# Sums of weight blocks made by adding transfers in DRAM, and the down product of an MLP taken form by form

## The chip, the cores and the metric

The program runs on one core of one Trainium2 chip. The metric is the device time in microseconds (us) of one execution. TensorE (PE) multiplies, VectorE (DVE), ScalarE (ACT) and GpSimd (POOL) do elementwise work, and SyncE (SP) issues nearly all transfers (DMAs). Every engine takes its instructions in the order of its own queue. Inputs, weights and intermediates that do not fit on the chip lie in DRAM.

## The reference

A trunk of two layers on 1024 tokens of width 1024. Cut to what matters:

```python
for i in range(2):
    mix = hgrn2_mixer(x, ...) if i == 0 else conformer_conv_mixer(x, ...)
    x = layer_norm(ALPHA * x + mix, ...)
    ff = square(relu(x @ ffn_w1[i])) @ ffn_w2[i]     # 1024 -> 4096 -> 1024
    x = layer_norm(ALPHA * x + ff, ...)
```

The first mixer is a gated linear recurrence over 8 heads (a projection, a recurrence in chunks, a norm with an output gate, an output projection). The second is a pointwise product, a causal convolution of 31 taps per channel, a norm and a second product. All numbers are float32, and the result must be that of float32.

## The kernel before, in words

**Products.** Each float32 operand is split into a high part (rounded to float32r) and a low part (the rest): ACT casts, DVE subtracts (`Slots.split`, line 67). `product` (line 298) then issues three matmuls of 128x128 by 512 columns: high by high, high by low, low by high.

**The down product by forms.** The second MLP product (hidden by `ffn_w2`) is done with seven block products in place of eight. The hidden layer is cut into 8 units of 512 (`NFC`), and each unit's 2 by 2 blocks of hidden activations and of weights are combined into seven forms, taken in the order `ORDER = (1, 2, 6, 5, 7, 3, 4)`. The forms of the hidden activations are written to DRAM by the up product (`hf`, by `store`, line 754) and loaded as tile `dh`. The forms of the weights are made on the chip, as tile `dw`: `Forms.unit` (line 122) loads a unit's four blocks, and DVE makes four sums (`Forms.add`, line 117: tiles `ds` and `dr`), before each form is split. `down_all` (line 850) works through four sets of two units each (`sets`). For each set and form it computes, for each of four groups `gi` (a half of the tokens and a row block in it), 12 matmuls into a PSUM bank. Banks `z` hold the running sum over forms 1, 6, 7, 4 and banks `w` that over 2 and then 5, 3. After every form of every set DVE adds the bank into the rows `y` (`into`, line 854). In the last set the forms 7, 3, 4 are taken group by group, so that the rows `after` them (`to_conv` in layer 0, `last_norm` in layer 1) can be normed one after the other. Four row blocks of 128 tokens make a half; forms 1, 2 and 4 end in blocks with n = 0 (t = 0, 1), and 6, 5, 7, 3 in blocks with n = 1 (t = 2, 3).

**Weights prepared ahead.** While the first MLP runs, `spare` (line 909) loads a weight block of the second mixer or of the second layer's first MLP product into `next`, splits it into `spare` and writes both parts to DRAM (`ready`), so that later it is loaded already split, by two transfers. `ahead` (line 673) lists 32 such blocks: 24 of the mixer and 8 of `w1`. `Forms.form` calls `spare` for 2 (up product) or 3 (down product) of every 7 forms. A `w1` block is used twice, once per half of the tokens (steps `UA` and `UB`); the 8 prepared ones serve steps 0 and 1 of both halves. Blocks without a prepared form are loaded into `raw` and split on the way.

**The recurrence** (line 449, per head and half of the tokens) ends with ACT writing an output tile `o`, which SP stores to `od`. During heads 4 to 7, and after the last one, `gates` (line 405) norms and gates the heads' outputs; in it POOL does two small operations per row block (lines 418 and 382), and DVE continues with their result.

**The order of the work.** Each engine's queue is ordered when the program is built, by a timeline simulated there (`schedule_with_timeline_sim=True`, line 1279); within that, `SEQ` (line 38) sets the order of steps in the second layer: `P` pointwise products, `N` and `F` the convolution's norm, `S` second product, `UA` and `UB` the up product of the two halves. The convolution's taps run beside it, 18 on DVE and 12 by way of POOL (`convolve`, `convolve_pool`, lines 1044 to 1094).

Of the kernel before, what the change touches and what calls it, by code (L numbers as in the profile page):

```python
# [15 lines left out]
P = 128  # L16
D = 1024
S = 1024
KB = D // P
# [37 lines left out]
class Slots:  # L57


    def __init__(self, nc, vector, slots, raws=None):  # L60
        self.nc, self.vector, self.slots, self.raws = nc, vector, slots, raws
        self.queue, self.todo, self.behind = [], [], []

# [7 lines left out]
    def load(self, pieces=1):  # L71

        src, slot = self.todo.pop(0), self.slots()
        self.queue.append(slot)
        if isinstance(src, tuple):
            for i in range(2):
                self.nc.sync.dma_start(out=slot[:, i].bitcast(F32), in_=src[i])
            yield
            return
        raw = self.raws() if self.raws else slot[:, 1].bitcast(F32)  # L80
        if self.behind:
            self.nc.gpsimd.tensor_copy(out=raw[:, :1], in_=self.behind.pop())
        step = 1024 // pieces
        for i in range(pieces):
            c = slice(i * step, (i + 1) * step)
            self.nc.sync.dma_start(out=raw[:, c], in_=src[:, c])
            self.split(slot, raw, c)
            yield

# [11 lines left out]
class Forms(Slots):  # L101


    def __init__(self, nc, vector, slots, raws, sums, spare=None, rate=0, skip=0):
        super().__init__(nc, vector, slots, raws)
        self.sums, self.spare, self.rate, self.skip, self.made = sums, spare, rate, skip, 0

    def form(self, raw):
        slot = self.slots()
        self.split(slot, raw)  # L110
        self.queue.append(slot)
        self.made += 1
        if self.made > self.skip:
            for _ in range(self.made * self.rate // 7 - (self.made - 1) * self.rate // 7):
                self.spare()
# [116 lines left out]
def body(ctx, tc, d, out):  # L232
# [162 lines left out]


# [52 lines left out]
    def recurrence(h, half, zq, zf, carry):  # L449
# [16 lines left out]
        nc.gpsimd.memset(g_r, 1.0)  # L466
# [88 lines left out]
        nc.sync.dma_start(out=od[h // 4][half][:, :, h % 4 * P : (h % 4 + 1) * P], in_=o)  # L555
        carry[h] = state
# [116 lines left out]
    ahead = [("wpw1", (j, i)) for j in range(KB) for i in (1, 0)] + [("wpw2", (n, k)) for n in range(2) for k in range(4)] + [("w1", (i,)) for i in range(8)]  # L673
# [85 lines left out]
    class Up:  # L759
# [9 lines left out]
        def put(self, hr, m, n, t, src, scale):  # L769
            nc.scalar.activation(t, src, AF.Relu, scale=scale)  # L770
            nc.scalar.activation(hr[:, m, n], t, AF.Square)
            mark[0] = hr[:, m, n, :1]
# [68 lines left out]


    mark = [None]
    sets = [(0, 1), (2, 3), (4, 5), (6, 7)]
# [5 lines left out]
    def down_all(y, fw, fh, copies, after, then=None):  # L850

        zs, xs = bank((0, 1, 2, 3)), bank((4, 5, 6, 7))

        def into(gi, m, n, ps, op=ALU.add):
            half, tb = divmod(gi, 2)
            yv = y[half][:, n * 2 + tb, m * HT : (m + 1) * HT]
            vector.tensor_tensor(out=yv, in0=yv, in1=ps, op=op)
            mark[0] = yv[:, :1]

        def one(gi, f, h, ps, start=True):  # L860
# [5 lines left out]
            product(ps, [(two(hp, tok(q)), two(fp, slice(q * HT, (q + 1) * HT))) for fp, hp in zip(f, h) for q in range(2)], start)  # L866


        place = {1: (0, 0, ALU.add), 2: (0, 0, ALU.add), 6: (0, 1, ALU.add), 5: (1, 1, ALU.subtract), 7: (1, 1, ALU.subtract)}
        place.update({3: (0, 1, ALU.add), 4: (1, 0, ALU.subtract)})  # L870
        def step(gi, i, f, h, z, w, copy=None):
            if i in (2, 5):
                w[gi] = xs()
            ps = w[gi] if i in (2, 5, 3) else z[gi]
            one(gi, f, h, ps, i in (1, 2, 5))
            m, n, op = place[i]
            if copy:
                t = copy()
                nc.scalar.copy(out=t, in_=ps)
                ps = t  # L880
            into(gi, m, n, ps, op)

        for s in sets:
            z, w, last = [zs() for _ in range(4)], [None] * 4, s == sets[-1]
            for i in ORDER[:4] if last else ORDER:
                f, h = fw.take(2), fh.take(2)
                fw.ahead(4)
                fh.ahead(4)
                for gi in range(4):
                    step(gi, i, f, h, z, w)  # L890
        f, h = {}, {}
        for gi in range(4):
            for i in ORDER[4:]:
                if gi == 0:
                    f[i], h[i] = fw.take(2), fh.take(2)
                step(gi, i, f[i], h[i], z, w, copies if i == 7 else None)
# [4 lines left out]
            half, tb = divmod(gi, 2)  # L901
            for end in [after(half, (1 - n) * 2 + tb) for n in range(2)][::-1]:
                if end:
                    end()
# [4 lines left out]
    def spare():  # L909
# [3 lines left out]
        slot, raw = hold  # L913
        if staged:
# [6 lines left out]
        if ahead:  # L921
            name, at = ahead.pop(0)

            nc.gpsimd.tensor_copy(out=raw[:, :1], in_=mark[0])
# [4 lines left out]
    fw = Forms(nc, vector, slots((144, 152, 48, 112, 120), "fw"), raws(run(192, 4, 4)), raws(run(160, 2, 4), "sum"), spare, 2)  # L929
# [36 lines left out]
    for half in range(2):  # L966
        for t in range(NTB):
            nc.sync.dma_start(out=y[half][:, t, :], in_=kept[half][t])
            nc.scalar.activation(y[half][:, t, :], y[half][:, t, :], AF.Copy, scale=ALPHA)
# [18 lines left out]
    dc = ring(run(0, 4, 2), wide_t, "dc")  # L988
# [4 lines left out]
    def plan_conv():  # L993
        for op, i in steps:
# [4 lines left out]
            elif op[0] == "U":  # L999
                wa.plan([ready.get(("w1", (4 * i + j,)), d["w1"][4 * i + j]) for j in range(4)])  # L1000
# [3 lines left out]
    down_all(y, fw, fh, dc, to_conv, plan_conv)  # L1004
# [156 lines left out]
    for op, i in steps:  # L1161
# [19 lines left out]
        else:  # L1181
# [3 lines left out]
            if i == NFC - 1:  # L1185
                fw = Forms(nc, vector, slots([64, 72, 144, 152, 200, 208, 112], "dw"), raws([132, 136, 140, 104, 108, 176, 180, 216], "dr"), raws([192, 196, 184, 188], "ds"))
# [28 lines left out]
    down_all(y, fw, fh, ring(run(0, 4, 2), wide_t, "dc"), last_norm)  # L1215
# [67 lines left out]
```

## Time and profile before

| | |
|---|---|
| median of 3 runs | 2159.1 us (2157.28 to 2162.01) |
| the profiled execution's own time | 2158.64 us |
| its span, first to last instruction | 2156.9 us |
| granted TensorE clock | 0.998 |
| DMA | 396.39 MB, mean 184 GB/s |

The stages, as the trace's PE rows show them: the recurrence and projections up to some 480 us, the output projection and first norm to 570, the first up product to 882, the first down product to 1193, the second layer's mixer and the first half of its up product to some 1570, the second half's to 1840, and the second down product from 1840 to 2144. In rows of instructions the first number is the start, the second the duration, and a bracket gives the engine's idle time before it and what ended it. In rows of groups the count is followed by the busy time in us and the mean duration in ns. In rows of waits stand the total, the number of waits and the longest, in us. In rows of transfers stand the count, the size of one and the median time from issue to landing.

### The profile page before, as it was taken

To read this page: it belongs to the slowest core of one execution; us is meant where nothing else is said; L and a number is where in the kernel's file an instruction comes from. 1 tells how busy PE (TensorE), PEld (TensorE's weight loads), DVE (VectorE), ACT (ScalarE), POOL (GpSimd) and SP (SyncE) were. 2 spreads that over 40 slices of the span, in tenths; PEclk is the share of its full clock that TensorE was granted. 3 is DMA by queue.
4 is the path that set the end of the run, shared out by engine and by line. 5 is a ranking of instruction groups with operands and counts; after the bars stand their busy time and mean duration, and the time that the engine had idled before them with its cause. 6 is when DMAs were issued, how large, how long until landed. Compare 5 with 4: busy or idle time off the path is not lost. (4 is left out here: it accounts for less than half of the span.)

```text
span 2156.9 us, 27191 instructions
## 1 busy us (share of the span) xinstructions
PE 2128.9 (99%) x10256; PEld 1769.4 (82%) x10256; DVE 1610.9 (75%) x2281; ACT 968.6 (45%) x1349; POOL 348.2 (16%) x324
## 2 busy tenths in 40 slices
PE   8999999999999999999999999999999999999997
PEld 7888888888888888888888888778788888888886
DVE  6667898876776666889887899579945344878777
ACT  4222332241256555645443576368653343433333
POOL 0000020021100000000001699089401000000001
PEclk9999999999999999999999999999999999999999
DMA  4101220331347767988873755553465988744422
GB/s 182 64 30 30 86 72 30 114 126 49 108 156 259 248 213 272 345 302 322 307 252 123 263 185 187 205 215 125 149 239 217 345 307 306 274 155 154 143 96 96
DMA packets 134978, 396.39 MB, mean 184 GB/s; under 512 B 12736, under 2 KB 41664, under 8 KB 133312
## 3 DMA queue, kind: packets, MB, share of 16 engines
q1 hardware_dynamic: 134848, 394.67, 51.9%
q8 instruction: 80, 1.31, 0.2%
q14 instruction: 50, 0.41, 0.1%
HBM read 277.18 MB, written 117.44 MB: 183 GB/s over the span
## 5 line engine op out<-in xcount | busy, mean ns | idle before, releaser
L167 PE MATMUL ps<-dw,dh 128*128 128x512 f32 x2688 | 610.6, 389 | 0.0
L167 PEld LDWEIGHTS ps<-dw,dh 128*128 128x128 f32 x2688 | 504.5, 188 | 104.4
L167 PE MATMUL ps<-x1f,fw 128*128 128x512 f32 x1344 | 308.1, 390 | 1.2 <-ACT fw L68 0.8
L167 PEld LDWEIGHTS ps<-x1f,fw 128*128 128x128 f32 x1344 | 251.4, 188 | 53.7 <-ACT fw L68 1.2
L167 PE MATMUL ps<-xa,wa 128*128 128x512 f32 x1152 | 270.5, 393 | 1.6 <-ACT xa L604 1.6
L167 PEld LDWEIGHTS ps<-xa,wa 128*128 128x128 f32 x1152 | 215.0, 189 | 45.7 <-ACT xa L604 2.0
L167 POOL TENSOR_TENSOR cb<-cb,prod 128x512 f32<-128x512 f32 x176 | 240.8, 1377 | 22.2 <-ACT prod L1057 11.5
L167 DVE SCALAR_TENSOR_TENSOR ps<-u,par,ps 128x512 f32<-128x512 f32 x288 | 198.5, 749 | 10.8 <-ACT ps L1067 9.5
L167 PE MATMUL ps<-x0T,wa 128*128 128x512 f32 x768 | 190.3, 398 | 6.3 <-ACT x0T L346 6.3
L167 DVE TENSOR_TENSOR y<-y,ps 128x512 f32<-128x512 f32 x232 | 156.5, 682 | 35.6 <-PE ps L167 35.1
L167 PE MATMUL ps<-xc,wa 128*128 128x512 f32 x768 | 174.2, 389 | 0.0
L382 POOL TENSOR_TENSOR mv<-mv,nhalf 128x1 f32<-128x1 f32 x32 | 44.7, 1399 | 780.5 <-DVE mv L167 780.5
L167 PEld LDWEIGHTS ps<-x0T,wa 128*128 128x128 f32 x768 | 141.9, 189 | 34.7 <-ACT x0T L346 6.3
L167 PEld LDWEIGHTS ps<-xc,wa 128*128 128x128 f32 x768 | 144.2, 188 | 29.9
L68 ACT CAST dh<-dh 128x1024 fp32r<-128x1024 f32 x112 | 117.3, 1052 | 114.5 <-DMA dh<-hf 112.9
L167 DVE TENSOR_TENSOR dh<-dh 128x1024 fp32r<-128x1024 f32 x112 | 136.0, 1222 | 25.3 <-ACT dh L68 24.7
L167 DVE TENSOR_TENSOR wa<-raw,wa 128x1024 fp32r<-128x1024 f32 (+1 forms) x74 | 96.6, 1307 | 75.4 <-ACT wa L68 75.3
L68 ACT CAST wa<-raw 128x1024 fp32r<-128x1024 f32 (+1 forms) x74 | 75.7, 1025 | 161.6 <-PE ps L167 140.1
L1057 ACT ACTIVATE prod<-u,par 128x512 f32<-128x512 f32 x176 | 124.4, 721 | 46.6 <-POOL cb L167 45.9
L167 PE MATMUL ps<-wv,x0T 128*128 128x512 f32 x576 | 142.0, 395 | 0.0
L167 PEld LDWEIGHTS ps<-wv,x0T 128*128 128x128 f32 x576 | 106.0, 188 | 21.3
L68 ACT CAST dw<-dr 128x1024 fp32r<-128x1024 f32 x64 | 67.1, 1052 | 88.3 <-PE ps L167 83.8
(178 smaller groups left out, 2791.7 us busy)
## 6 DMA issues: line engine op xcount, KB each, us to landing
wa<-ready SPq DMA_DIRECT2D x128, 512.0 KB, 4.4
dh<-hf SPq DMA_DIRECT2D x112, 512.0 KB, 4.7
ready<-spare SPq DMA_DIRECT2D x64, 512.0 KB, 3.8
dr<-in_w_dram SPq DMA_DIRECT2D x64, 512.0 KB, 5.3
raw<-in_w_dram SPq DMA_DIRECT2D x48, 512.0 KB, 5.0
raw<-in_w1q_dram SPq DMA_DIRECT2D x36, 512.0 KB, 3.8
hf<-ht SPq DMA_DIRECT2D x64, 256.0 KB, 4.2
hf<-ht SPq DMA_DIRECT2D x32, 512.0 KB, 7.0
```

Source lines behind the costliest of these rows:

```text
L68: self.nc.scalar.copy(out=slot[:, 0, c], in_=raw[:, c])
L167: return op(*args, **kw)
L382: nc.gpsimd.tensor_tensor(out=dst, in0=src, in1=nhalf[:, :n], op=ALU.pow)
L1057: nc.scalar.activation(tp, u[:, k : k + HT], AF.Copy, scale=tap(j, k))
```

## The change

- **Sums in DRAM.** A new helper is called once at the end of each of the 16 recurrence steps, for one of the 16 units (8 per layer). It makes the four sums of the unit's weight blocks in DRAM: two copies on SP's queue, then three transfers on POOL's queue that add into their destination. A transfer of two numbers from `o` goes first, so that the copies start only after that step's output.
- **Down product form by form.** `down_all` runs over forms on the outside and over all 8 units inside; each bank gathers a form over 8 units before DVE adds it into `y`. Each form of the weights is loaded from DRAM, from an input block or a sum, and split (`Slots` in place of `Forms`). Form 4 takes two units for all groups, then the other six group by group. The blocks with n = 1 are normed after form 3, those with n = 0 after each group.
- **Rows loaded later.** `y` (the residual) of layer 0 is loaded and scaled when the third unit of form 1 is taken, not before the down product.
- **Preparing weights.** `ahead` lists 13 `w1` blocks in place of 8, and they are used in `UA` only. `spare` is called for 3 of 8 forms in the up product up to the 43rd, and 5 of 8 in the down product from the 12th to the 55th; its load now follows the split of the form just loaded, by a one-column copy on DVE and one on POOL.
- **Smaller edits.** The memset of `g_r` in the recurrence goes from POOL to ACT. In the last rows, blocks (1,0) and (1,1) in place of (1,1) and (1,3) take the norm by statistics on DVE.

```diff
+    def block_sums(name, layer, c, after):
+        t = sums[name, layer, c] = dram.tile([4, P, 1024], F32, name=f"sum_{name}{layer}{c}")
+        v, w = t.rearrange("a p n -> p a n"), d[name][layer, c].rearrange("a p n -> p a n")
+        nc.sync.dma_start(out=t[0:4:2, 0, 0:1], in_=after)
+        nc.sync.dma_start(out=v[:, 0:2], in_=w[:, 0:4:2])
+        nc.sync.dma_start(out=v[:, 2:4], in_=w[:, 0:2])
+        nc.gpsimd.dma_start(out=v[:, 0:2], in_=w[:, 2:4], accum_op=ALU.add)
+        for i in (2, 3):
+            nc.gpsimd.dma_start(out=v[:, i], in_=v[:, i - 1], accum_op=ALU.add, max_dma_last_dim=4096)
+    def form(name, layer, c, i):
+        w, t = d[name][layer, c], sums[name, layer, c]
+        return {1: w[0], 2: w[1], 6: t[2], 5: t[1], 7: t[0], 3: t[3], 4: w[3]}[i]
...
-        nc.gpsimd.memset(g_r, 1.0)
+        nc.scalar.activation(g_r, f_l, AF.Identity, bias=one, scale=0.0)
...
         nc.sync.dma_start(out=od[h // 4][half][:, :, h % 4 * P : (h % 4 + 1) * P], in_=o)
+        block_sums(*to_sum.pop(0), o[:2, 0, :1])
...
     def plan_down(layer, fw, fh):
-        fw.todo = [[(blocks("w2", layer, c),) for c in s] for s in sets]
-        fh.plan([hf[layer][c][i] for s in sets for i in ORDER for c in s])
+        fw.plan([form("w2", layer, c, i) for i in ORDER for c in range(NFC)])
+        fh.plan([hf[layer][c][i] for i in ORDER for c in range(NFC)])
...
+        for i in ORDER:
+            for c in range(NFC if i != 4 else 2):
+                f, h = fw.take(), fh.take()
+                if c == 2 and i == 1 and first:
+                    first(f[0][:, 1, :1].bitcast(F32))
                 fw.ahead(4)
                 fh.ahead(4)
                 for gi in range(4):
+                    one(gi, i, f, h, c == 0 and i in (1, 2, 5))
+                    if c == NFC - 1:
+                        into(gi, i)
+            if i == 3:
+                rings["aux"] = bank((4, 5))
+                rows = [lambda gi=gi: after(gi // 2, 2 + gi % 2) for gi in range(4)]
+                for _ in range(2 if then else 4):
+                    rows.pop(0)()
+        f, h = fw.take(NFC - 2), fh.take(NFC - 2)
         for gi in range(4):
+            for c in range(0, NFC - 2, 2):
+                one(gi, 4, f[c : c + 2], h[c : c + 2])
+            into(gi, 4)
...
+            end = after(gi // 2, gi % 2)
...
-ahead = [("wpw1", (j, i)) for j in range(KB) for i in (1, 0)] + [("wpw2", (n, k)) for n in range(2) for k in range(4)] + [("w1", (i,)) for i in range(8)]
+ahead = [("wpw1", (j, i)) for j in range(KB) for i in (1, 0)] + [("wpw2", (n, k)) for n in range(2) for k in range(4)] + [("w1", (i,)) for i in range(13)]
...
-    fw = Forms(nc, vector, slots([112, 120, 144, 152, 128, 136, 168], "dw"), raws([192, 196, 200, 204, 160, 164, 64, 68], "dr"), raws([80, 84, 88, 92], "ds"), spare, 3)
+    fw = Slots(nc, vector, slots([112, 120, 144, 152, 128, 136, 168], "dw"), raws([192, 196, 200, 204, 160, 164], "dr"), spare, 5, range(12, 56))
...
-                wa.plan([ready.get(("w1", (4 * i + j,)), d["w1"][4 * i + j]) for j in range(4)])
+                wa.plan([ready.get(("w1", (4 * i + j,)) if op == "UA" else None, d["w1"][4 * i + j]) for j in range(4)])
...
-        if (half, t) not in ((1, 1), (1, 3)):
+        if (half, t) not in ((1, 0), (1, 1)):
```

More of the change, by code (lines that the diff above doesn't have):

```diff
@@ L88, in load, with count @@
             yield
+        self.count(slot)
+    def count(self, slot):
+        if self.spare:
+            self.made += 1
+            if self.made in self.when and self.made * self.rate // 8 > (self.made - 1) * self.rate // 8:
+                self.spare(slot[:, 1, :1].bitcast(F32))
     def ahead(self, n):
@@ L111, in form @@
         self.queue.append(slot)
[L112 to L115, printed above, removed]
+        self.count(slot)
     def add(self, x, y, out=None):
@@ L864, in tok, with into @@
                 return slice(q * HT + half * 256 + tb * P, q * HT + half * 256 + (tb + 1) * P)
[L866 to L875, printed above, removed]
-            m, n, op = place[i]
[L877 to L886, printed above, removed]
+            parts = [(two(hp, tok(q)), two(fp, slice(q * HT, (q + 1) * HT))) for fp, hp in zip(f, h) for q in range(2)]
+            product((w if i in (2, 5, 3) else z)[gi], parts, start)
+        def into(gi, i):
+            half, tb = divmod(gi, 2)
+            m, n, op = place[i]
+            yv = y[half][:, n * 2 + tb, m * HT : (m + 1) * HT]
+            vector.tensor_tensor(out=yv, in0=yv, in1=(w if i in (2, 5, 3) else z)[gi], op=op)
+        for i in ORDER:
[3 more added lines that the diff above has]
+                    first(f[0][:, 1, :1].bitcast(F32))
                 fw.ahead(4)
@@ L900, in down_all, with spare @@
                 then()
[L901 to L904, printed above, removed]
+            end = after(gi // 2, gi % 2)
+            if gi == 1:
+                while rows:
+                    rows.pop(0)()
+            if end:
+                end()
     hold, staged = [], []
-    def spare():
+    def spare(after):
         if not hold:
```

58 lines of the change are left out of this document (26 added, 32 removed).

## The prediction

> **What bounds the kernel now.** I read the page first, then who PE (TensorE) waited for, then stretches of the span (after the stretch: busy us and instruction count of PE, weight loads, DVE, ACT and POOL; granted clock; DMA share; GB/s), then single places.
>
> ```profile
> span 2156.9 us, 27191 instructions
> PE 2128.9 (99%) x10256; PEld 1769.4 (82%) x10256; DVE 1610.9 (75%) x2281; ACT 968.6 (45%) x1349; POOL 348.2 (16%) x324
> ...
> PE ps L167 <- ACT x0T L346: 6.3, 1, 6.3
> PE ps L167 <- DVE cb L167: 3.5, 2, 2.9
> PE ps L167 <- ACT xa L604: 1.8, 3, 1.3
> ...
> 72.00:455.00 383.00, 382.33 (x2333) 323.86 (x2332) 301.74 (x622) 106.77 (x174) 17.63 (x29) 1.00 0.21 67
> ...
> 928.00:1135.00 207.00, 207.00 (x915) 171.47 (x914) 183.75 (x198) 98.06 (x96) 19.43 (x17) 1.00 0.81 287
> ...
> 1839.60:2144.40 304.80, 304.80 (x1345) 252.15 (x1343) 238.86 (x270) 128.66 (x136) 7.24 (x5) 1.00 0.45 153
> ```
>
> PE is the bound nearly everywhere. In the second layer's down product (last row) 1345 matmuls take 304.8 us, 226 ns each, with DVE free for a fifth of the time. The change has the same 1344 matmuls of 512 columns per layer, so neither fewer DVE additions nor fewer DVE sums can shorten that stretch by themselves. What can be won at all is PE's idle time, 2156.9 - 2128.9 = 28 us: the 6.3 at the start, which the change does not touch, about 12.5 at the end, and what is left in the convolution. So I price three places where the end can move: the last rows, the convolution, and the places where new transfers may make PE wait.
>
> **The tail.**
>
> ```profile
> 2139.71 4.70 PE L167 MATMUL ps<-dw,dh 128*128 128x512 f32 x20
> ...
> 2145.64 0.63 DVE L167 TENSOR_TENSOR y<-y,ps 128x512 f32<-128x512 f32 x1
> 2146.19 1.27 DVE L167 SCALAR_TENSOR_TENSOR y<-y,mv,ln_ffn_b 128x1024 f32<-128x1024 f32 x1
> ...
> 2148.77 0.68 DVE L167 BATCH_NORM_STATS2 bs<-y 128x6 f32<-128x512 f32 x1
> 2149.37 1.39 DVE L167 SCALAR_TENSOR_TENSOR y<-y,mv,ln_ffn_b 128x512 f32<-128x512 f32 x2
> 2150.69 0.20 DVE L167 BATCH_NORM_AGGREGATE mv<-bs 128x2 f32<-128x12 f32 x1
> 2150.92 0.15 DVE L167 TENSOR_SCALAR mv<-mv 128x1 f32<-128x1 f32 x1
> 2150.99 1.40 DVE L167 SCALAR_TENSOR_TENSOR y<-y,mv,ln_ffn_g 128x512 f32<-128x512 f32 x2
> 2152.31 1.41 DVE L167 SCALAR_TENSOR_TENSOR y<-y,mv,ln_ffn_b 128x512 f32<-128x512 f32 x2
> ```
>
> Columns: start, duration. PE ends at 2139.71 + 4.70 = 2144.41; DVE ends at 2152.31 + 1.41 = 2153.72, so 9.3 us of DVE follow the last product, because three row blocks are in their norm at once. After the change the four blocks of n = 1 are normed from form 3's end on, beside form 4's 192 matmuls, and block (1,0) runs under the last 36 of them (36 x 0.226 = 8.1 us); behind the last product stands one block: add 0.63, statistics 0.68, 0.20 and 0.15, first pass 1.40, second pass 1.41 (POOL's power lies under the first pass), together 4.5, and some 0.3 for the releases between engines: 4.8. **Gain 4.5.** Bounds: 4.8 without those releases, and 2.0 if two more passes (1.40 + 1.41) still stand ahead of it on DVE. The first of those four groups of 36 also takes six units in 8.1 us, each with two splits of 1.22 on DVE (a row below); the two units ahead of it (48 matmuls, 10.8 us) are the cover, and 6 x 2.44 = 14.6 us fit into 18.9; the norms beside them may push PE back by up to 2, inside the lower bound. The store after it is the same.
>
> **The convolution.** Here w1 blocks 0 to 12 are split in advance instead of 0 to 7, and used in the first half only.
>
> ```profile
> 1540.72 0.39 PE L167 MATMUL ps<-xa,wa 128*128 128x512 f32 x1
> 1544.04 0.66 PE L167 MATMUL ps<-ident,cb 128*128 128x128 f32 x4 [2.93 <-DVE cb L167]
> 1544.45 2.95 PE L167 MATMUL ps<-xa,wa 128*128 128x512 f32 x8
> 1547.20 1.05 PE L167 MATMUL ps<-ident,cb 128*128 128x128 f32 x4
> ...
> 1541.10:1548.00 6.90, 3.97 (x18) 0.81 0.25 77
> ...
> 1432.00:1541.00 109.00, 108.40 (x488) 89.33 (x486) 101.11 (x132) 86.72 (x134) 98.09 (x67) 1.00 0.41 139
> 1545.00:1640.00 95.00, 95.00 (x437) 78.71 (x436) 58.46 (x87) 42.13 (x64) 4.06 (x3) 0.98 0.51 185
> ...
> L167 DVE TENSOR_TENSOR wa<-raw,wa 128x1024 fp32r<-128x1024 f32 x15 | 26.8, 1785 | 3.3 <-ACT wa L68 3.3
> ```
>
> Before 1541 DVE is busy for 101 of 109 us and POOL for 98; PE then stands for the convolution's sums and its clock falls (0.81 in that stretch). From 1541.10 to 1548.00 there are 10 matmuls and 8 transposes: at 226 ns, and 100 ns per transpose (four from 1544.04 to 1544.45), 3.1 us of work in 6.9. So 3.8 are lost, and 3.5 - 2.9 = 0.6 more in an earlier wait for cb. The change takes 13 - 8 = 5 splits out of the first half: 5 x 1.785 = 8.9 us of DVE, more than the wait. **Gain 4.4.** Bounds 0 (POOL's additions end last instead) and 6.2 (the waits for xa, 1.8, too). The second half gains 8 splits, 8 x 1.8 = 14 us at most, in a stretch where DVE is busy for 58 of 95: no cost, and without that cover 14.
>
> **The recurrence.** Each of 16 steps gets on SP's queue one tiny transfer and two copies of 1 MB, and on POOL's one addition of 1 MB and two of 512 KB, each waiting for the one before. POOL stands in its queue at those waits; behind them are the gates' small operations.
>
> ```profile
> 71.82 0.60 ACT L554 ACTIVATE o<-ps 128x512 f32<-128x512 f32 x1 [2.12 <-PE ps L167]
> ...
> 451.98 0.60 ACT L554 ACTIVATE o<-ps 128x512 f32<-128x512 f32 x1
> ...
> 273.63 0.19 POOL L418 TENSOR_SCALAR ss<-ss 128x4 f32<-128x4 f32 x1 [2.23 <-DVE ss L167]
> ...
> 472.00 1.01 POOL L382 TENSOR_TENSOR ss<-ss,nhalf 128x4 f32<-128x4 f32 x1
> ...
> ha<-ha SPq DMA_DIRECT2D x8, 1024.0 KB, 5.3
> ...
> raw<-in_wqf_dram SPq DMA_DIRECT2D x14, 512.0 KB, 3.6
> ...
> od<-o SPq DMA_DIRECT2D x16, 256.0 KB, 2.6
> ...
> y<-in_x_dram SPq DMA_DIRECT2D x2, 2048.0 KB, 8.0
> ...
> 273.28 0.40 ACT L465 COPY G<-F 128x256 f32<-128x256 f32 x1
> ```
>
> First and last of 16 outputs o: a step each (451.98 - 71.82) / 15 = 25.3 us. No row shows an adding transfer. Lower bound, as a plain transfer: tiny 2.6, copies 8.0 at the worst, additions 5.3 and 3.6 until the last is issued: 19.5. Upper, an addition at twice a plain one: 2.6 + 8.0 + 10.6 + 7.2 = 28.4. DMA is busy at 0.21 from 72 to 455, so the room is there, and the sums are first needed after 885. SP's queue stands some 2.6 us per step at the tiny transfer; loads of the next head behind it are a step early. What can cost time is POOL: the gates' operations (16 pairs between 273.63 and 473) sit in POOL's queue between the additions, DVE waits for each of them in its own order, and PE for DVE. The queue's order is fixed at the build by a simulated timeline (line 1279); an addition longer than assumed there holds what follows, by up to 28.4 - 19.5 = 8.9 in each of the four or so steps that share POOL with the gates: 0 to +36. I take **+2**, nearer the lower end, since POOL is busy for 18 of 383 us there. The memset that goes from POOL to ACT lengthens the chain of G by some 0.4, 16 x 0.4 = 6.4 if bare; PE is fed from other products there (382.3 of 383 busy): 0.
>
> The Trainium skill (Collectives: The Full Stack, The bandwidth ceiling) says that an add in the transfer engines reads two sources through one ring and so runs at half a copy's rate; no run here shows it. By that rule the chain would be the upper one, 28.4, longer than a step, and the first rival below decides.
>
> **The first down product.** DVE loses 84 of 112 additions and 32 sums per layer, and gets 7 more splits of weights in advance.
>
> ```profile
> L167 DVE TENSOR_TENSOR y<-y,ps 128x512 f32<-128x512 f32 x232 | 156.5, 682 | 35.6 <-PE ps L167 35.1 <-POOL next L924 0.3
> ...
> L167 DVE TENSOR_TENSOR ds<-ds,dr 128x1024 f32<-128x1024 f32 x32 | 39.0, 1221 | 0.2
> ...
> L167 DVE TENSOR_TENSOR spare<-next,spare 128x1024 fp32r<-128x1024 f32 x32 | 39.1, 1223 | 20.5 <-ACT spare L916 20.4
> ...
> dh<-hf SPq DMA_DIRECT2D x50, 512.0 KB, 6.0
> ...
> SPq L920 <- ACT spare L916: 66.0, 18, 8.6
> SPq L86 <- PE ps L167: 53.1, 24, 9.2
> ```
>
> That is 84 x 0.682 + 32 x 1.22 - 7 x 1.22 = 88 us of DVE per layer here and 96 in the last, all beside a PE that never waits: 0. Accumulation in PSUM across eight units adds no wait, since a bank that DVE reads at the end of a form is written again a form (43 us) later. Transfers grow: a unit and form is 24 x 0.226 = 5.4 us and loads 2 x 512 KB; from the 12th load to the 50th, 207 us, 25 steps of preparing load 512 KB and store 1 MB. 39 x 1.05 + 25 x 1.57 = 80 MB in 207 us is 387 GB/s, where the stretch 928:1135 moved 287 at a share of 0.81, or 354 at a full one. So the queue ends some 9% of 207, 19 us, late. SP now waits for PE to free dh slots (53.1 us), so it runs ahead to the seven slots: six units, 32 us, less 6.0 and 2.3 of split leaves 24 of cover. **0**; without that cover +19.
>
> **Sum.** 2158.64 (this execution's time, 1.7 above its span) - 4.5 - 4.4 + 2 = 2151.7. The median of the runs, 2159.1, is 0.5 higher: **2152**.
>
> **Rivals.**
> *POOL is held in the recurrence* (slower). Place: gates behind an addition; it decides when a chain exceeds what the order allowed by more than about 5 us in four or five steps, 5 x 5 = 25 net of the 2: 2152 + 23 = 2175. For it: PE has no wait to lose there, and every late DVE result becomes a PE wait. Against it: 25.3 us a step against 19.5.
> *Transfers bound the first down product* (slower): the 19 us come without cover, because SP stands at 25 stores instead of 18: 2171. For it: 387 against 354. Against it: the slots.
> *The convolution's wait stays*: POOL's 98 of 109 us are not relieved, so 2152 + 4.4 = 2156.4.
> *The change does not do what it says* at the end: the last block still finds DVE occupied by norms and splits, so its gain is the lower bound or less: 2152 + 4.5 = 2156.5. For it: DVE was busy in the last rows above without a gap. Against it: 84 additions fewer.
>
> **How the numbers follow.** Forecast 0.47 (own range 2146 to 2156), convolution 0.14, tail 0.06, POOL 0.20, transfers 0.13. This measurement tells about 0.2%, 4.3 us, from no change: under 2154.8 is faster, over 2163.4 slower. The forecast gives 0.43 to faster and 0.04 to same; the next two 0.07 and 0.11, with 0.02 slower; the last two 0.33 slower. Together 0.50, 0.15, 0.35. Low end: 2152 with the upper bounds of tail (0.3) and convolution (1.8), nothing lost in the recurrence (2) and 3 won there (POOL's queue without the memset that DVE waits on): 2145. The high end takes in both slower cases at their prices and leaves out the upper part of POOL's bound: 2178.
>
> **What will show it.** Right: PE's last matmul some 8.5 us before the last instruction's end instead of 12.5; no wait for cb over 1 us near the end of the first half's w1; PE busy to 0.5 us in each stretch from 72 to 500; full PE in the first down product at a DMA share above 0.9. Wrong: PE waits for yn or state between 270 and 480, POOL's small operations far behind their DVE releasers, or PE waiting for dw or dh splits between 930 and 1140.

## The result and the profile after

The changed kernel takes 2172.65 us (median of 6, 2170.48 to 2178.47) against 2159.22 us for the kernel before beside it: ratio 1.0065, 95% interval 1.005 to 1.0079. It is slower by 0.65%, and the forecast was 2152, faster. The time lies inside the stated range; the direction is the other one, and the number is 2.4 us from the 2175 of the rival *POOL is held in the recurrence*.

The profiled execution of after took 2172.09 us. Its waits of PE (total, number, longest) and its stretches, columns as in the prediction:

```profile
PE ps L172 <- DVE yn L172: 14.9, 1, 14.9
...
PE ps L172 <- ACT z L1150: 1.8, 2, 1.2
PE ps L172 <- ACT xa L631: 1.4, 1, 1.4
```

```profile
72.00:250.00 178.00, 177.34 (x1059) 150.31 (x1057) 125.93 (x247) 50.98 (x83) 16.57 (x17) 1.00 0.75 189
250.00:400.00 150.00, 149.69 (x928) 126.40 (x927) 135.51 (x294) 46.06 (x82) 28.31 (x33) 1.00 0.85 219
400.00:450.00 50.00, 50.00 (x313) 42.32 (x313) 34.84 (x75) 10.87 (x18) 5.72 (x6) 1.00 1.01 305
450.00:500.00 50.00, 34.38 (x156) 27.92 (x155) 22.58 (x48) 16.95 (x27) 16.87 (x22) 0.83 0.93 259
```

One new wait of 14.9 us, in the only stretch where PE lost its work, and there the clock fell to 0.83. From 72 to 500 us the DMA share is 0.75 and more (0.21 before, up to 455), and from 400 on the engines are full or nearly so (1.01, then 0.93).

Marks set on the first product of each stage show where the time went. In all traces of this study they are read at the same five places; "no sums" and "moved" are the experiments e3 and e12 below.

| us | before | after | no sums | moved |
|---|---|---|---|---|
| start to first x1f,fw (recurrence, output projection, first norm) | 571.87 | 591.57 | 571.95 | 575.65 |
| from there to first xa,wa (first MLP) | 621.53 | 621.05 | 621.00 | 621.03 |
| to the second dw,dh (convolution, second up product) | 646.20 | 645.38 | 645.38 | 645.96 |
| to the last product's end | 304.81 | 304.81 | 304.80 | 304.80 |
| to DVE's last instruction | 9.31 | 4.53 | 4.54 | 4.53 |

So +19.7, -0.5, -0.8, 0, -4.8: together +13.6, and the spans differ by 13.4. All of the loss is in the first row.

What PE waited for is seen on three engines' timelines of after (start, duration, engine, line; the bracket is the idle time before and what ended it). POOL:

```profile
444.84 1.19 POOL L410 DMA_DIRECT2D sum_w<-in_w_dram  x1 [10.90 <-DMA sum_w<-in_w_dram]
457.29 0.86 POOL L412 DMA_DIRECT2D sum_w<-sum_w  x1 [11.26 <-DMA sum_w<-in_w_dram]
466.63 0.81 POOL L412 DMA_DIRECT2D sum_w<-sum_w  x1 [8.48 <-DMA sum_w<-sum_w]
467.25 1.41 POOL L410 DMA_DIRECT2D sum_w<-in_w_dram  x1
483.93 0.86 POOL L412 DMA_DIRECT2D sum_w<-sum_w  x1 [15.26 <-DMA sum_w<-in_w_dram]
484.87 0.19 POOL L444 TENSOR_SCALAR ss<-ss 128x4 f32<-128x4 f32 x1
485.14 1.03 POOL L387 TENSOR_TENSOR ss<-ss,nhalf 128x4 f32<-128x4 f32 x1
```

DVE, then PE:

```profile
465.96 1.28 DVE L172 TENSOR_REDUCE ss<-sq 128x4 f32<-128x512 f32 x2 [8.77 <-ACT sq L441]
...
486.21 1.14 DVE L172 SCALAR_TENSOR_TENSOR yn<-yn,ss,sg 128x128 f32<-128x128 f32 x4 [16.70 <-POOL ss L387]
```

```profile
467.65 4.01 PE L172 MATMUL ps<-wa,x0T 128*128 128x512 f32 x17
486.61 0.74 PE L172 MATMUL ps<-ident,yn 128*128 128x128 f32 x2 [14.95 <-DVE yn L172]
487.00 3.76 PE L172 MATMUL ps<-wa,x0T 128*128 128x512 f32 x8
```

DVE had the sums of squares ready at about 467. POOL's two small operations on them (lines 444 and 387, 1.2 us) stand in its queue behind the second addition of a unit, and that one waits for the first, from 467.25 to 483.9. PE ran out of other products at 471.66. The eight matmuls after the wait take 470 ns each where 226 is usual (granted clock 0.50 from 486.5 to 491). In numbers: the first ident,yn product starts at 439.87 before and 442.70 after (+2.8), the wait is 14.95, and some 2 us more go to the low clock.

The chain of waits of after tells the same from the other end (start, duration, what):

```profile
423.60 12.15 DMA sum_w<-o
435.81 8.64 DMA sum_w<-in_w_dram
...
444.84 11.87 DMA sum_w<-in_w_dram
...
457.29 0.86 POOL sum_w L412
...
467.25 16.28 DMA sum_w<-in_w_dram
...
484.87 0.20 POOL ss L444
...
486.21 0.36 DVE yn L172
486.57 0.04 issue
486.61 121.96 PE ps L172 x587
```

### The profile page after: what moved, and what is told of

Same layout as the page of the kernel before. It is cut to its first block, busy times and chain, and to the rows that moved or that the text cites. A ratio compares the mean times of both kernels' runs of the same rounds, so it can differ in the third digit from the quotient of the medians.

```text
span 2170.3 us, 27318 instructions
## 1 busy us (share of the span) xinstructions
PE 2133.8 (98%) x10256; PEld 1772.7 (82%) x10256; DVE 1452.6 (67%) x2098; ACT 973.4 (45%) x1365; POOL 378.9 (17%) x369
## 2 busy tenths in 40 slices
DMA packets 161349, 494.99 MB, mean 228 GB/s; under 512 B 15040, under 2 KB 43968, under 8 KB 159680
## 3 DMA queue, kind: packets, MB, share of 16 engines
HBM read 370.50 MB, written 189.79 MB: 258 GB/s over the span
## 4 chain that ended last, share of the span: by engine, by line
PE 91%; DMA 4%; DVE 2%; POOL 1%; issue 1%; ACT 1%; SPq 0%; DVEq 0%; POOLq 0%; ACTq 0%
PE ps L172 91%; DMA sum_w<-in_w_dram 2%; POOL cb L172 1%; DMA sum_w<-o 1%; DVE wa L172 0%; DMA raw<-in_w_dram 0%; DVE ps L172 0%; DMA raw<-in_wg_dram 0%; DMA raw<-in_wv_dram 0%; DMA raw<-in_wqf_dram 0%; DVE wv L172 0%; DMA raw<-in_xT_dram 0%; DMA raw<-in_w1q_dram 0%; ACT wv L69 0%; ACT wa L69 0%
## 5 line engine op out<-in xcount | busy, mean ns | idle before, releaser
L172 DVE TENSOR_TENSOR dw<-dr,dw 128x1024 fp32r<-128x1024 f32 x112 | 136.6, 1222 | 110.6 <-ACT dw L69 110.0
L69 ACT CAST dw<-dr 128x1024 fp32r<-128x1024 f32 x112 | 117.4, 1052 | 133.1 <-PE ps L172 124.8
L172 DVE TENSOR_TENSOR wa<-raw,wa 128x1024 fp32r<-128x1024 f32 (+1 forms) x77 | 96.8, 1258 | 88.6 <-ACT wa L69 88.2
```

Of the source, the lines that this page charges most:

```text
L69: self.nc.scalar.copy(out=slot[:, 0, c], in_=raw[:, c])
L172: return op(*args, **kw)
```

## Experiments

Times are medians; each has its interval against the kernel before on the same chip where it matters. "Mark" means the first row of the table, which is 571.9 before and 591.6 after; it and the waits come from the one profiled execution of a run, which can lie some us from the median. "Marker" is the transfer of two numbers that goes ahead of a unit's copies. Two explanations compete in the expectations below. *Hold*: POOL stands at the wait of an addition, with the gates' operations behind it in its queue. *Traffic*: the DMA engines are full, so that o and yn come late whatever POOL does.

### What in the recurrence costs: the sums, their adding, or their bytes

**e3, no sums.** The call is dropped; forms 6, 5, 7 and 3 load plain blocks.

```diff
-        block_sums(*to_sum.pop(0), o[:2, 0, :1])
...
-        return {1: w[0], 2: w[1], 6: t[2], 5: t[1], 7: t[0], 3: t[3], 4: w[3]}[i]
+        return {1: w[0], 2: w[1], 6: w[2], 5: w[1], 7: w[0], 3: w[3], 4: w[3]}[i]
```

> Leaves the sums out: forms 6, 5, 7 and 3 of the second weights take plain input blocks; all else is the changed kernel. If the sums in the recurrence are the whole loss: span before 450 us as in the kernel before, no wait for yn, tail and convolution as in the changed kernel, total 2152 to 2155. If the rest of the change (forms one by one, marks of the spare work, copies) costs as well: 2157 or more.

2152.38 us (2151.6 to 2153.36), ratio 0.9972 (0.9962 to 0.9982), mark 571.95. All of the loss comes from making the sums; the rest of the change is worth 6.7 us.

**e4, plain copies.** POOL's three transfers per unit lose `accum_op=ALU.add`; queue, chain, places and sizes stay, and the adding is left out.

> Leaves the adding out: POOL's three transfers per unit write the same places by plain copies, same queue, same chain, same bytes moved to the destination. If the hold is long because an addition takes about half as long again as a copy (10.4 against 6.8 us for 1 MB): the three transfers of the last units end some 8 to 10 us earlier, PE's wait for yn falls to 3 to 7 us, total 2160 to 2165. If it is long because each waits for the one before on full DMA engines, adding or not: the wait stays at 11 to 15 us, total 2168 to 2173.

2153.55 us, ratio 0.998 (0.9971 to 0.999), mark 574.03: better than either expectation. The queues and issues of after, then of e4 (packets, MB, share of 16 engines; then count, size, median us from issue to landing):

```profile
q0 software_dynamic: 8960, 33.56, 8.7%
...
sum_w<-in_w_dram POOLq DMA_DIRECT2D x16, 1024.0 KB, 10.4
sum_w<-sum_w POOLq DMA_DIRECT2D x32, 512.0 KB, 5.5
```

```profile
q0 software_dynamic: 8960, 33.56, 4.5%
...
sum_w<-in_w_dram POOLq DMA_DIRECT2D x16, 1024.0 KB, 7.0
sum_w<-sum_w POOLq DMA_DIRECT2D x32, 512.0 KB, 3.8
```

The same packets and bytes hold the engines for 8.7% of 2170.3 us instead of 4.5% of 2151.9: 188.8 against 96.8 us of all 16, a factor of 1.95, or 178 against 347 GB/s. That is the price that the prediction left open between 1 and 2. The Trainium skill (Collectives: The Full Stack, The bandwidth ceiling) says that an add runs at half a copy's rate because it reads two sources. The rate is what this pair of runs shows; the reason is not, since the profile's page counts the same reads from memory in both (370.50 MB).

**e2, gates off POOL.** The additions stay; the second gates' two small operations go to DVE and ACT.

```diff
+            if n == 0:
...
+            else:
+                vector.tensor_scalar(out=ss[:, 1], in0=ss[:, 0], scalar1=1.0 / P, scalar2=RMS_EPS, op0=ALU.mult, op1=ALU.add)
+                nc.scalar.activation(ss[:, 1], ss[:, 1], AF.Sqrt)
+                vector.reciprocal(ss[:, 0], ss[:, 1])
```

> All sums stay where the changed kernel makes them; only the second gates' two small operations leave POOL's queue (DVE multiplies and adds, ACT takes the root, DVE the reciprocal). Hold theory: POOL stands as long as in the changed kernel (its additions near 457, 467 and 484 us), but nothing of PE waits for it; PE's wait for yn falls from 14.9 to under 3 us, total 2154 to 2159. Traffic rival (yn's loads from DRAM are late behind full queues, whichever engine does the gates): the wait stays above 8 us, total 2164 to 2171.

2160.09 us, ratio 1.0024 (1.0009 to 1.0038). The executions fall in two groups, four from 2159.3 to 2160.1 and three from 2167.3 to 2168.4; the profiled one is of the upper. In it the wait for yn is gone, and another stands in its place:

```profile
473.09 1.15 ACT L441 ACTIVATE sq<-yn 128x512 f32<-128x512 f32 x2 [14.00 <-DMA yn<-od]
480.62 0.60 ACT L438 ACTIVATE sg<-ps 128x512 f32<-128x512 f32 x1 [6.38 <-issue]
```

```profile
481.99 6.09 PE L172 MATMUL ps<-wa,x0T 128*128 128x512 f32 x14 [11.92 <-DVE sg L172]
```

ACT stands 14 us for yn's load from DRAM, and then 6.38 more before `sg`, for which PE waits; that the profile puts down to nothing ("issue"). In after, the same instruction waited for the store of the last o:

```profile
467.00 0.60 ACT L438 ACTIVATE sg<-ps 128x512 f32<-128x512 f32 x1 [0.55 <-DMA od<-o]
```

In e2 that store is issued at 459.44, and SP issues the load of yn that needs it at 480.56, just before `sg` starts. So it is most likely this store, some 21 us under way, that PE waits for; no run shows it alone. Two things then end close together: POOL's hold, and o's way through DRAM to yn on full engines. Taking the first away wins some 12 us in one group and 5 in the other, of which only the second has a trace. Both theories had a part: the hold is the longer of the two, the traffic the one right behind it.

### Which units

**e6, last three copied; e7, only the last three added.** In e6 units 5 to 7 of layer 1 are copied without adding, in e7 the other thirteen.

```diff
+        op = {"accum_op": ALU.add} if (layer, c) < (1, 5) else {}
-        nc.gpsimd.dma_start(out=v[:, 0:2], in_=w[:, 2:4], accum_op=ALU.add)
+        nc.gpsimd.dma_start(out=v[:, 0:2], in_=w[:, 2:4], **op)
```

> Leaves the adding out for the last three units alone (plain copies at the same places); thirteen units are added as in the changed kernel. Local theory (only the additions beside the loads of yn and y at 400 to 490 us cost): PE's wait for yn falls under 2 us, total 2153 to 2157. Backlog theory (each addition is a little late, and the lateness of thirteen adds up to the hold): the wait stays at 8 us or more, total 2164 to 2172.

> The reverse: thirteen units are plain copies, the last three are added. Local theory: PE's wait for yn stays at 10 to 16 us, total 2166 to 2173. Backlog theory: the wait falls under 3 us, total 2153 to 2158.

e6: 2169.49 us (two executions near 2163, three near 2170; the profiled one waits 7.6 for yn and 2.7 for sg). e7: 2162.43 us (seven from 2159.8 to 2164.4, three from 2169.0 to 2170.4; 7.0 for sg). Neither theory holds alone: the last additions cost some 9 us by themselves (e7 against e4), and earlier ones make even plain copies late (e6). The stores of o in after say why it is the end. SP's queue:

```profile
379.93 0.56 SPq L581 DMA_DIRECT2D od<-o  x1
399.21 0.56 SPq L581 DMA_DIRECT2D od<-o  x1
422.98 0.57 SPq L581 DMA_DIRECT2D od<-o  x1
442.20 0.57 SPq L581 DMA_DIRECT2D od<-o  x1
...
455.03 0.56 SPq L581 DMA_DIRECT2D od<-o  x1
```

The last steps are 19.3, 23.8, 19.2 and 12.8 us long, not the mean of 25.3, and in them the residual's 4 MB are loaded too. A unit whose additions alone take 10.4 and 5.5 us at the median, and up to 16.3 there, is started every 12.8 to 23.8 us: the units pile up just where the second gates need POOL.

### Moving the last three units

**e1, in the first up product.** Called after units 5 to 7 of that product, marked by a weight slot.

```diff
-        block_sums(*to_sum.pop(0), o[:2, 0, :1])
+        if len(to_sum) > 3:
+            block_sums(*to_sum.pop(0), o[:2, 0, :1])
...
+        if c >= NFC - 3:
+            block_sums(*to_sum.pop(0), f[:2, 1, :1].bitcast(F32))
```

> The sums of the last three units (layer 1, c 5 to 7) are made in the first up product, the other thirteen in the recurrence as in the changed kernel. Hold theory (the additions of the last units stand ahead of the second gates' two small operations in POOL's queue, and PE stands 14.9 us for yn behind them): the wait of PE for yn falls under 1.5 us, PE keeps its clock there, first x1f,fw product 16 to 19 us earlier than 591.6, total 2153 to 2157. Traffic rival (the transfers as such keep yn's loads and POOL late): a wait of 8 us or more stays, total 2164 to 2171. Rival that the added bytes cost wherever they are put: the up product takes as much longer as the recurrence saves, total 2168 to 2173.

2170.71 us; no wait for yn, mark 576.82, but the first MLP takes 638.5 instead of 621.0 (the profiled execution took 2174.84 us). The last rival's number came out, yet not because bytes cost everywhere:

```profile
PE ps L172 <- ACT dh L69: 5.0, 1, 5.0
PE ps L172 <- DVE c L172: 3.9, 1, 3.9
PE ps L172 <- ACT c L823: 2.7, 2, 2.0
```

They met the loads of weights prepared ahead and the first loads of dh, for which ACT stands in order (11.0 us for dh at 889.66).

**e5, in the second down product, unmarked; e8, the last three unmarked at their old place.** Both leave the marker out for these units; the edit shown is e8's.

```diff
-        nc.sync.dma_start(out=t[0:4:2, 0, 0:1], in_=after)
+        if (layer, c) < (1, 5):
+            nc.sync.dma_start(out=t[0:4:2, 0, 0:1], in_=after)
```

> The sums of the last three units are made in the second down product during its first form, which needs none of them (the share of the DMA engines there was 0.56 and POOL has next to nothing to do), without a marker transfer. Hold theory with a local cause: no wait of PE for yn, none in the first up product, the recurrence loses 2 to 5 us, the second down product nothing: total 2153 to 2157. Rival that the additions' bytes cost wherever they are put: PE waits for dw or dh in the second down product for 8 us or more, total 2163 to 2172.

> The marker transfer is left out for the last three units, so that SP does not stand some 12 us until it has landed and the copies start at once after the store of o. If the wait for the marker is part of the hold's length: the last additions end 8 to 12 us earlier, PE's wait for yn falls to 3 to 7 us, total 2160 to 2165. If the transfers are bound by the DMA engines, which are full from 400 to 490 us, the order in which they are issued changes little: wait 11 to 16 us, total 2168 to 2174.

2164.43 and 2165.69 us. Neither tested what it was made for: with nothing to wait for, the three units' additions ran at 24 to 75 us in both, whatever their place in the program, since the build's simulated timeline orders the queues. There they delayed a small load, and in e8

```profile
54.52 0.72 DVE L172 COPY_PREDICATED at<-mask,ps 128x512 f32<-128x512 int32 x1 [9.83 <-DMA mask<-in_mask_dram]
```

so that PE stood 7.4 us for qn (6.7 in e5). The wait for yn was gone in both: with the last units away, the hold is too. Without a marker nothing pins a unit to its place.

**e9, in the second down product, marked.** As e5, with `f[0][:2, 1, :1]` as marker.

> As e5, but with a marker transfer from the weight slot in use, so that the three units start in the second down product and not elsewhere. If the hold of POOL in front of the second gates is the loss: wait for yn under 1 us, first x1f,fw product at 573 to 577 us, second down product without waits, total 2153 to 2157. Rival that the second down product has no room for them (three units of about 18 us of all engines in its first 87 us): PE waits for dw or dh 5 us or more, total 2160 to 2170.

2170.38 us. Mark 577.08, first MLP 621.04, but 661.2 in the convolution and second up product: two units were issued at 1685 to 1728 us, ahead of the down product, and PE stood 6.1 and 2.0 us for wa there. (Of the 15.8 us more in that row, 3.8 are products of the down product taken early: its own row is that much shorter.) A place that is free by its own share says nothing of the one where the transfer is issued.

**e12, in the second up product.** After blocks 1, 3 and 5 of its first half; in the recurrence as in e1.

```diff
...
             up_half(1, i, 0, wa, stA, x3T[0])
+            if i in (1, 3, 5):
+                block_sums(*to_sum.pop(0), wa.queue[0][:2, 1, :1].bitcast(F32))
```

> The last three units are made in the first half of the second up product, one after every second block, where POOL has 7 us of work in 300 and the DMA engines' share is 0.72. If the hold in front of the second gates is the loss and traffic costs nothing where there is room: no wait for yn, none in the second up product, total 2153 to 2157. If the share rises to 1 there and weights come late: 2160 to 2170.

2156.87 us, ratio 1.000 (0.999 to 1.0009): 15.8 us less than after, with the same transfers. No wait for yn; last column of the table. This is the clearest proof that the last three units, at their place, were most of the loss. 3.7 us of the first row stay.

### The 4 us that stayed

**e13, layer 0's sums alone,** in the first eight steps (the second layer's are left out). **e15,** e12 with all gates off POOL as in e2.

```diff
+        if to_sum[0][1] == 0:
             block_sums(*to_sum.pop(0), o[:2, 0, :1])
```

> Sums of layer 0 alone, made in the first eight steps of the recurrence, before any gate; the second layer's forms 6, 5, 7 and 3 take plain input blocks (its sums are left out). Hold theory (additions cost only where the gates' operations stand behind them): first x1f,fw product at 572 to 573 us, total 2152 to 2154. Traffic theory (each unit costs some 0.25 us wherever it stands in the recurrence): 574 us and later, total 2154.5 to 2157.

> As e12 (thirteen units in the recurrence, three in the second up product), with the two small operations of all gates off POOL's queue (DVE, ACT root, DVE reciprocal). Hold theory: first x1f,fw product at 572 to 573.5 us instead of 575.7, total 2153 to 2155. Traffic theory: it stays at 575 to 577, total 2156 to 2158.

2156.61 and 2158.8 us (e15: ratio 1.000), marks 577.69 and 576.51: the hold theory misses both. e15 weighs less, since its square root makes ACT load function tables 20 times in place of twice, 1.28 us each. e13 shows that this loss arises before any gate. ACT in e13, what it stood for:

```profile
87.33 1.05 ACT L69 CAST wv<-raw 128x1024 fp32r<-128x1024 f32 x1 [4.98 <-DMA raw<-in_wv_dram]
...
242.18 1.05 ACT L69 CAST wv<-raw 128x1024 fp32r<-128x1024 f32 x1 [11.15 <-DMA raw<-in_wg_dram]
```

In e3 the same two places show 1.2 and 4.0. The units started after steps 0 and 5 (stores of o at 72.6 and 223.6) run just ahead of two bursts of weight loads; ACT's casts come late, then DVE's splits, and PE stands 2.7 us for qn at 242.9.

**e16, none after steps 0 and 5.** Eleven units in the recurrence; five in the last pointwise block and after blocks 1, 3, 5 and 7.

```diff
+        if 2 * h + half not in (0, 5, 13, 14, 15):
             block_sums(*to_sum.pop(0), o[:2, 0, :1])
```

> Eleven units in the recurrence (none after steps 0 and 5, which stand ahead of the two bursts of weight loads, none after the last three), five in the last pointwise block and the second up product. If weights that come late behind these two units are what is left of the loss: no wait of PE for qn over 0.3 us, first x1f,fw product at 572 to 573.5 us, total 2152.5 to 2155, faster than the kernel before. If every unit costs a little wherever it stands: 574.5 us and more, total 2155.5 to 2159. If five units are too many for the end of the convolution: waits for cb, z or xa there, total above 2158.

2161.71 us, ratio 1.0018 (1.0009 to 1.0027). Mark 573.16 and no wait of PE between 72 and 400 us: that was most of the recurrence's remaining loss (e3: 571.95). But the convolution takes 653.6 us instead of 645.4:

```profile
PE ps L172 <- DVE cb L172: 7.9, 2, 6.2
```

POOL makes cb there, and additions between its taps are the same hold in another place: POOL stood 5.4 and 3.0 us before the issues at 1494 and 1514.

**e17, two of those later:** after blocks 1, 3, 5, 6 and 7.

> Eleven units in the recurrence as in e16, five in the second up product after blocks 1, 3, 5, 6 and 7. If e16's loss in the convolution was the unit in the last pointwise block: no wait for cb over 1.5 us, total 2152.5 to 2155.5, faster than the kernel before by 0.1 to 0.25%. Rival that units closer together than some 30 us hold each other and the weights up there: waits in the second up product or for cb, total 2156 to 2162.

2161.18 us (2157.91 to 2165.0), ratio 1.0015. Mark 573.56 again, 653.0 after it: 2.9 us for cb and 3.2 for a wa loaded already split. Its rival held.

**e14, layer 1's units in the convolution:** five among the pointwise blocks, three as in e12, layer 0's in the first eight steps.

> All sixteen sums: layer 0 in the first eight steps of the recurrence, layer 1 in the convolution (after every second pointwise block, five units) and in the second up product (three units, as in e12). If only the hold in front of the gates costs: total 2152 to 2155, faster than both kernels. Rival: the convolution's own work on POOL (46 of 50 us busy there) stands behind the additions, PE waits for cb or xa: 3 us or more in the convolution, total 2157 to 2166.

2167.83 us, ratio 1.0046. The convolution loses 7.8 us (waits of 5.5 for z and 2.7 for cb), the recurrence 4.7: the rival again, with a median above its 2166. No version tried with the sums beats the kernel before; e12 and e15 equal it.

### The two smaller terms

**e10, list of 8; e11, norms of rows moved back.** Both without sums, as e3.

```diff
-... + [("w1", (i,)) for i in range(13)]
+... + [("w1", (i,)) for i in range(8)]
```

```diff
-                for _ in range(2 if then else 4):
+                for _ in range(2):
...
+            if gi > 1 and rows:
+                rows.pop(0)()
...
-            if gi == 1:
+            if gi == 1 and then:
```

> Leaves the sums out like e3, and the list of weights split ahead goes back from 13 to 8 blocks of the second first-layer weights. If the longer list is what shortened the convolution: the wait for cb at its second half returns (2 to 3 us), total 0.5 to 1.5 us above e3's 2152.4. If the list does nothing there and the convolution's small gain comes from elsewhere: within 0.4 us of e3.

> Leaves the sums out like e3, and two of the last norms go back behind the last products' groups 2 and 3. If moving those norms ahead is what shortened the end: DVE's last instruction ends 7 to 9 us after the last product as in the kernel before, total 2155 to 2157. If the earlier additions of the products into y did it: within 1 us of e3's 2152.4.

e10: 2154.47 us, 2.1 above e3; the third row of the table is 647.5 against 645.4, with cb at 2.8 us in place of 0.5. e11: 2153.19 us; DVE ends 5.1 us after the last product, against 4.5. So the list is worth about 2 us, more than the 0.5 to 1.5 expected, and its wait is the one expected. Of the shorter end, these two norms are worth 0.6 us; the other 4.2 belong to what e11 leaves in place, probably the additions made form by form and earlier, which no run tried alone.

## Why the prediction was wrong

**The tail** was forecast at -4.5 and measured -4.8. Right in size, and one block of DVE work stands behind the last product, as said; the norms moved ahead, named as the means, had a small part in it (e11). In after:

```profile
2162.84 0.69 DVE L172 TENSOR_TENSOR y<-y,ps 128x512 f32<-128x512 f32 x1 [3.67 <-PE ps L172]
...
2165.93 1.41 DVE L172 SCALAR_TENSOR_TENSOR y<-y,mv,ln_ffn_b 128x512 f32<-128x512 f32 x2
```

The bracket of 3.67 says that DVE was waiting for PE there; before, it ran without a gap.

**The convolution** was forecast at -4.4 and measured -0.8. The named wait did go (cb 3.5 to 0.6 in total), so the mechanism held. The size did not, and missed what came next:

```profile
1386.75 0.66 PE L172 MATMUL ps<-ident,y 128*128 128x128 f32 x4 [1.16 <-ACT z L1150]
...
1389.19 6.73 PE L172 MATMUL ps<-wa,xa 128*128 128x512 f32 x22 [0.44 <-ACT r L1051]
...
1453.13 9.82 PE L172 MATMUL ps<-xa,wa 128*128 128x512 f32 x35 [1.38 <-ACT xa L631]
```

The last transposes of y now stand one behind the other instead of among other products, the wait for z grew from 0.7 to 1.8 us, and the clock falls after these short waits (0.86 from 1385 to 1397, 0.83 from 1453 to 1463: 22 matmuls in 6.73 us, 35 in 9.82; at 226 ns each 5.0 and 7.9). In the kernel before it fell after the long wait for cb, and stayed at 1.00 after the same wait for xa:

```profile
1431.11 0.97 PE L167 MATMUL ps<-xa,wa 128*128 128x512 f32 x3 [1.32 <-ACT xa L604]
...
1432.27 37.23 PE L167 MATMUL ps<-xa,wa 128*128 128x512 f32 x163
```

The waits of that part fell from 7.3 to 5.1 us, but the part is only 0.8 shorter, so 1.4 of those 2.2 were lost again, in the main to slow matmuls. With the list back at 8 blocks (e10) this part takes 647.5 us, 1.3 more than before the change: by these executions the list won 2.1 of the 4.4 forecast, and the rest of the change, which had no term there, cost 1.3. The longer wait for z is no doing of the list alone, since e10 has 1.4 of it. What brought about the new order is not shown.

**The first down product** was forecast at 0, with the queue late but covered. Right: the first MLP is 0.5 us shorter, PE has 350.00 of 350 us between 900 and 1250 at a DMA share of 0.91. The fear of 19 us (*transfers bound the first down product*) did not come true. The splits in the second half were free, as said (PE is busy for 300.00 of 300 us from 1570 to 1870).

**The recurrence is the step that failed:** "I take **+2**, nearer the lower end, since POOL is busy for 18 of 383 us there", within bounds of 0 to +36. It cost 19.7. Four things in that step were wrong:

- The reason did not bear on the question. POOL's busy time counts its instructions; what blocks the queue is standing at a wait, and POOL stood 15.26 us before one issue.
- The price was taken near a plain transfer's. Measured, an addition takes 10.4 us for 1 MB and 5.5 for 512 KB, against bounds of 5.3 to 10.6 and 3.6 to 7.2: the first at the upper end, the second in the middle, and 16 us on full engines. The rule of the Trainium skill quoted in the prediction spoke for the upper end. With plain copies at the same places (e4) the mark grew by 2.2 us, which is the size of the +2.
- "The room is there" was read from the mean share of 0.21. With the sums the share is 1.01 from 400 to 450, and the unit whose marker was issued at 423.60 came to its last issue on POOL at 466.63: a chain of 43.0 us, beyond the upper bound of 28.4.
- "A step each 25.3 us" was a mean over steps of 12.8 to some 40 us. The trace before already had the last stores of o 18.3 and 11.2 us apart, into which a chain of 19.5 us, the lower bound itself, does not fit:

```profile
423.07 0.52 SPq L555 DMA_DIRECT2D od<-o  x1
...
441.40 0.53 SPq L555 DMA_DIRECT2D od<-o  x1
...
452.61 0.52 SPq L555 DMA_DIRECT2D od<-o  x1
```

The sign named for it came as written: PE waits for yn between 270 and 480 (from 471.66 on), and POOL's small operations are 17 us behind DVE's release. The rival *POOL is held in the recurrence* had the place right, and the price by luck: it expected several holds of 5 us, and it was a single one of 15, at the last units, with o's way through DRAM to yn right behind it. What the change is worth without that step, 2152.4 in e3, is the forecast's number by chance: what the convolution did not give makes up for the +2 left out, the tail's 0.3 and the first MLP's 0.5.

## What to carry to other kernels

A transfer that is "hidden" must be fitted into the stage's shortest steps and beside its busiest stretch, not its mean; an adding transfer counts twice in engine time. An engine that issues a waiting transfer stands for it, so look for the smallest operation queued behind it and for who needs that one; a low busy share says nothing about this. Moving the transfers to a stretch with a low DMA share helps only if no engine there has in-order work behind them: of the other places tried here, only those of e12 were nearly free.

## What the runs showed of the hardware

- An adding DRAM-to-DRAM transfer holds the DMA engines 1.95 times as long as a plain copy with the same records: packets (161349), bytes (494.99 MB) and the profile page's memory reads (370.50 MB) are identical in after and e4, so the count of bytes does not show it, only the share does. The mixed runs lie in between as their additions do: 173 us of all engines in e6 (thirteen units added) and 117 in e7 (three), where proportion gives 172 and 114.
- A transfer of two numbers behind full engines took 12.2 us in after (issued on SP at 423.60, the copies behind it at 435.81); but for one small load, SP's queue issued nothing in that time.
- The granted clock fell after waits that are short one by one: 1.16, 0.68 and 0.44 us within 4 us before the 22 slow matmuls above. After a wait of 1.38 us for xa it fell to 0.83 in after, and after one of 1.32 at the same place it stayed at 1.00 before; what decides was not tried. The Trainium skill (TensorE: Matmul & The Clock Gate, Part 1) has the array at half rate by default and after an idle window of about 3.4 us; no single wait there was that long, while the 14.95 us in the recurrence, with a clock of 0.50 behind them, fit it.
- The same program ran in two groups of times some 5 to 8 us apart (e2, e6, e7), probably because two chains end close together there, while e3 stayed within 1.8 us over nine executions. What decides between the groups was not tried.
